# Softmax cross-entropy gradient on one core: rows dealt to partitions 64 at a time instead of 2 at a time

## The chip, the cores and the metric

The kernel runs on one core of one Trainium2 chip. The metric is the device time of one execution in microseconds. Three runs of the kernel before took 1279.22, 1292.99 and 1301.48 us; the median is 1292.99 us.

## The reference

The logits are 8 x 1024 rows of 8192 numbers in fp32 (32 KB a row, 268.4 MB in all), and there is one label for each row. The result is the softmax of each row with 1 taken off at the label's column:

```python
def reference(logits, labels):
    logits_max = np.max(logits, axis=-1, keepdims=True)
    exp_logits = np.exp(logits - logits_max)
    softmax = exp_logits / np.sum(exp_logits, axis=-1, keepdims=True)
    one_hot = np.zeros_like(logits)
    one_hot[batch_idx, seq_idx, labels] = 1.0
    return (softmax - one_hot).astype(np.float32)
```

Every logit is read once and every result written once: 268.4 MB each way.

## The kernel before

**Tiling.** The 8192 rows are cut into 32 blocks (B) of 256 rows. A block holds two rows (G = 2) for each of 128 partitions (P), 64 KB in each partition and 8 MB in all. The tile X has three buffers for blocks (SLOTS), so that one block can be loaded, one worked on and one stored. A column of 128 rows, one in each partition, is called t; there are T = 64 of them, and t = 2b + j is row j of the pair in block b. Which rows of memory a partition gets is said in one place, the views x_b and o_b, in which p is the partition, b the block and j the row of the pair:

```python
x_b = x_nv.rearrange("(b p j) v -> b p j v", p=P, j=G)
o_b = o_nv.rearrange("(b p j) v -> b p j v", p=P, j=G)
```

Here b is the slowest index: a block is 256 consecutive rows, and partition p holds rows 256b + 2p and the one after it, 64 KB that lie together in memory.

**Pieces.** Three strings give, for every block, how it is loaded (LOADS), stored (STORES) and in which order its work is issued (ORDER). A block marked "w" is moved in one transfer of 128 x 64 KB; "r" in two, one for each j, of 128 x 32 KB; "s", for the loads of the first three blocks, in four, which take every second partition of one j. 24 blocks are loaded and 23 stored as "w"; the others are at the two ends.

**Queues.** All loads are issued by SP, but for half of the "s" pieces, which ACT issues at the start. All stores are issued by ACT. The function load waits until the stores from the same buffer, three blocks earlier, have landed; store waits for the last DVE operation of its rows. SP issues only loads, so a load that waits holds up only later loads.

**Work on one t.** row_max takes the negated maximum on DVE. exponentials makes exp(x - max) in place on ACT, with the sum beside it. mark writes a one-hot row of bytes into PSUM (the tile hot) with two ACT operations from the label's column: away is the distance of each group of four columns from the label's group (word), and hot gets the unit of the right byte at distance 0. finish takes the reciprocal of the sum on DVE, and one DVE operation multiplies the row by it and subtracts the bytes. The order is written out by hand in the last loop. All instructions go through the helper run, so the profile gives nearly all of them as line 76 (L76).

**Labels.** Before the first block, ACT's queue loads the labels into 32 partitions, 256 of them each (lab_raw, labels are 64-bit numbers). DVE casts them to fp32 (lab_f), TensorE transposes them twice against an identity matrix that POOL made with a memset and an affine_select, into PSUM (lab_ps, a corner of hot), and DVE casts them back into lab, 128 partitions x 64. From there small DVE operations make word, unit and minus, a column of numbers for each t. POOL's iota makes the column counter count16.

Of the kernel before, what the change touches and what calls it, by code (L numbers as in the profile page):

```python
# [7 lines left out]
P = 128  # L8
G = 2
# [8 lines left out]
def kernel(  # L18
# [6 lines left out]
    nc = tc.nc  # L25
    fp32 = mybir.dt.float32
    i32 = mybir.dt.int32
# [4 lines left out]
    Alu = mybir.AluOpType  # L32

    x_nv = logits.flatten_outer_dims()
    o_nv = out.flatten_outer_dims()
    N, V = x_nv.shape
    T = N // P
    B = T // G
    W = V // 4
    lab_bp = labels.rearrange("a b -> (a b)").rearrange("(b q) -> b q", q=G * P)  # L40
    x_b = x_nv.rearrange("(b p j) v -> b p j v", p=P, j=G)
    o_b = o_nv.rearrange("(b p j) v -> b p j v", p=P, j=G)

    const = ctx.enter_context(tc.tile_pool(name="const", bufs=1))
    psum = ctx.enter_context(tc.tile_pool(name="psum", bufs=1, space=bass.MemoryType.PSUM))

    X = const.tile([P, SLOTS, G, V], fp32)
    lab_raw = const.tile([B, G * P], labels.dtype)
    lab_f = const.tile([B, G, P], fp32)
    ident = const.tile([B, B], fp32)  # L50
    lab = const.tile([P, G, B], i32)
    part = const.tile([P, G, B], i32)
    word = const.tile([P, G, B], fp32)
# [5 lines left out]
    m, s, r = (const.tile([P, T], fp32, name=n) for n in ("m", "s", "r"))  # L59

    hot = psum.tile([P, G, W], i32)
    lab_ps = hot[:, 0, :].bitcast(fp32)[:, :T].rearrange("p (j b) -> p j b", j=G)

    with tc.tile_critical():  # L64
        sem = tc.alloc_semaphore
        got = [[sem(f"got{i}{q}") for q in range(4)] for i in range(SLOTS)]
        put = [[sem(f"put{i}{q}") for q in range(4)] for i in range(SLOTS)]
        lab_got, dve, act, pe, pool = (sem(n) for n in ("lab_got", "dve", "act", "pe", "pool"))
        count = {}

        def run(engine, waits, counter, method, **operands):

            waits = list(dict.fromkeys(waits))
            for w in waits[:-1]:
                engine.wait_ge(*w)  # L75
            instruction = getattr(engine, method)(**operands)  # L76
            for w in waits[-1:]:
                instruction._wait_ge(*w)
            step = 16 if method == "dma_start" else 1
            instruction.then_inc(counter, step)  # L80
            count[counter.name] = count.get(counter.name, 0) + step
            return counter, count[counter.name]
# [20 lines left out]
        def load(b):  # L103
            loaded[b] = []
            before = stored.get(b - SLOTS, [])
            for q, piece in enumerate(PIECES[LOADS[b]]):
                ps, js = piece
                free = [w for other, w in before if meets(piece, other)]
                queue = nc.scalar if LOADS[b] == "s" and ps == halves[1] else nc.sync
                w = run(  # L110
                    queue, free, got[b % SLOTS][q], "dma_start",
                    out=X[ps, b % SLOTS, js, :], in_=x_b[b, ps, js, :],
                )
                loaded[b].append((piece, w))
# [57 lines left out]
                )  # L172
            finished[t] = freed[t] = last

        w_raw = run(nc.scalar, [], lab_got, "dma_start", out=lab_raw[:], in_=lab_bp)
        for b in range(SLOTS):
            load(b)
        w = run(nc.gpsimd, [], pool, "memset", ap=ident[:], constant=0.0)
        w_ident = run(
            nc.gpsimd, [w], pool, "affine_select",  # L180
            out=ident[:], in_=ident[:], compare_op=Alu.not_equal, fill=1.0,
            base=0, pattern=[[-1, B]], channel_multiplier=1,
        )
        w_made = run(
            nc.gpsimd, [], pool, "iota", out=count16[:], pattern=[[1, W]], base=0, channel_multiplier=0
        )
        step = mybir.dt.size(labels.dtype) // 4
        lab32 = lab_raw[:].bitcast(i32).rearrange("b (p j s) -> b j p s", j=G, s=step)
        w_lab = run(nc.vector, [w_raw], dve, "tensor_copy", out=lab_f[:], in_=lab32[:, :, :, 0])
        for j in range(G):  # L190
            w = run(
                nc.tensor, [w_ident, w_lab], pe, "transpose",
                out=lab_ps[:, j, :], in_=lab_f[:, j, :], identity=ident[:],
            )
        w = run(nc.vector, [w], dve, "tensor_copy", out=lab[:], in_=lab_ps)
        w = run(
            nc.vector, [w], dve, "tensor_scalar",
            out=part[:], in0=lab[:], scalar1=2, scalar2=None, op0=Alu.arith_shift_right,
# [3 lines left out]
            out=word[:], in0=part[:], scalar1=-1.0, scalar2=None, op0=Alu.mult,  # L202
        )
        w = run(
            nc.vector, [w_word], dve, "tensor_scalar",
            out=lab[:], in0=lab[:], scalar1=3, scalar2=None, op0=Alu.bitwise_and,
        )
        w = run(
            nc.vector, [w], dve, "tensor_copy", out=minus[:], in_=lab[:]
        )  # L210
        powers = [256.0**k for k in range(4)]
        w = run(
            nc.vector, [w], dve, "tensor_scalar",
            out=unit[:], in0=minus[:], scalar1=0.0, scalar2=powers[0], op0=Alu.is_equal, op1=Alu.mult,
        )
        for k in (1, 2, 3):
            w = run(
                nc.vector, [w], dve, "tensor_scalar",
                out=part[:].bitcast(fp32), in0=minus[:], scalar1=float(k),
                scalar2=powers[k], op0=Alu.is_equal, op1=Alu.mult,  # L220
            )
            w = run(
                nc.vector, [w], dve, "tensor_tensor",
                out=unit[:], in0=unit[:], in1=part[:].bitcast(fp32), op=Alu.add,
            )
        made_dve = run(
            nc.vector, [w], dve, "tensor_scalar",
            out=minus[:], in0=unit[:], scalar1=-1.0, scalar2=None, op0=Alu.mult,
# [77 lines left out]
```

## Time and profile before

| what | value |
|---|---|
| median of three runs | 1292.99 us |
| the profiled execution, its time | 1284.52 us |
| its span, first to last instruction | 1282.7 us |
| DVE busy | 1120.0 us (87%) |
| ACT busy | 722.8 us (56%) |
| packets of the two DMA queues | 98.8% of 16 engines' span |
| moved | 536.98 MB, 419 GB/s over the span |

The profile is of one execution, whose time is 1.8 us longer than its span. Its queue q1 is that of SP, q10 that of ACT. A packet is one run of memory that one of the 16 DMA engines moves: 64 KB for a "w" piece, 32 KB for the others. The DMA share is the time in which packets were under way, as a mean over the 16 engines.

### The profile page before, as it was taken

The numbers are of one execution on the slowest core, as the hardware profiler recorded it, in microseconds if no ns is written. First come the engines' busy times: TensorE is split into PE (matmuls) and PEld (weight loads), VectorE is DVE, ScalarE is ACT, GpSimd is POOL, SyncE is SP. The second block draws the span as 40 slices with busy tenths as digits, with TensorE's granted clock in tenths as the row PEclk, the third lists the DMA queues.
The fourth block names the chain that finished last, engine by engine and source line by source line (L and its number), as shares of the span: only waits on it lengthen the run. The fifth ranks groups of instructions, "written<-read, shape, count | busy, mean of one in ns | idle before, by whom it ended". The sixth has DMA issues, their size and how long they took to land.

```text
span 1282.7 us, 759 instructions
## 1 busy us (share of the span) xinstructions
PE 0.4 (0%) x2; PEld 0.3 (0%) x2; DVE 1120.0 (87%) x207; ACT 722.8 (56%) x257; POOL 2.3 (0%) x7
## 2 busy tenths in 40 slices
PE   0000000000000000000000000000000000000000
PEld 0000000000000000000000000000000000000000
DVE  5999998797979899887997798896799859999995
ACT  2857666456545566544755456563655436656662
POOL 0000000000000000000000000000000000000000
DMA  9999999999989999999999999999999999999999
GB/s 394 425 433 450 425 426 452 425 396 419 454 358 388 441 425 427 425 425 425 425 417 423 380 382 439 442 378 394 425 413 386 443 423 427 410 436 430 436 428 391
DMA packets 11813, 536.98 MB, mean 419 GB/s; under 512 B 1408, under 2 KB 1408, under 8 KB 1440
## 3 DMA queue, kind: packets, MB, share of 16 engines
q10 hardware_dynamic: 6432, 281.09, 51.3%
q1 hardware_dynamic: 5376, 255.86, 47.5%
q14 instruction: 5, 0.04, 0.0%
HBM read 268.50 MB, written 268.44 MB: 419 GB/s over the span
## 4 chain that ended last, share of the span: by engine, by line
DMA 58%; DVE 33%; issue 6%; ACT 1%; DVEq 0%; ACTq 0%; SPq 0%
DMA X<-in_logits_dram 31%; DMA out_dram<-X 28%; DVE m L76 17%; DVE X L76 16%; ACT X L76 1%; DVEq L64 0%; DVE r L76 0%; ACT hot L76 0%; ACT away L76 0%; ACTq L76 0%; DVEq L75 0%; ACTq L301 0%; SPq L64 0%
## 5 line engine op out<-in xcount | busy, mean ns | idle before, releaser
L76 DVE TENSOR_REDUCE m<-X 128x1 f32<-128x8192 f32 x64 | 553.6, 8680 | 142.0 <-DMA X<-in_logits_dram 142.0
L76 ACT ACTIVATE X<-X,m 128x8192 f32<-128x8192 f32 x64 | 455.8, 7121 | 337.5 <-DVE m L76 337.5
L76 DVE SCALAR_TENSOR_TENSOR X<-X,r,hot 128x8192 f32<-128x8192 f32 (+1 forms) x65 | 560.0, 8616 | 3.8 <-ACT hot L76 1.6
L76 ACT ACTIVATE away<-count,word 128x2048 bf16<-128x2048 int16 x64 | 128.1, 2001 | 191.1 <-DVE X L76 149.9
L76 ACT ACTIVATE hot<-away,unit,minus 128x2048 int32<-128x2048 bf16 x64 | 131.9, 2062 | 2.1
L76 ACT ACTIVATION_READ_ACCUMULATOR X<-X,m 128x1 f32 x64 | 11.9, 186 | 0.0
L76 DVE RECIPROCAL r<-s 128x1 f32<-128x1 f32 x64 | 9.9, 154 | 0.0
L76 ACT ACT_TABLE_LOAD x1 | 1.3, 1283 | 5.3 <-issue 5.3
L76 DVE CAST lab_f<-lab_raw 32x256 f32<-32x256 int32 x1 | 0.5, 474 | 2.8 <-DMA lab_raw<-in_labels_dram 2.8
L76 POOL IOTA count<- 128x2048 int16 x1 | 1.8, 1823 | 0.0
L76 DVE TENSOR_TENSOR unit<-unit,part 128x64 f32<-128x64 f32 x3 | 0.7, 224 | 0.1
L76 DVE TENSOR_SCALAR part<-minus 128x64 f32<-128x64 f32 x3 | 0.6, 195 | 0.1
L76 DVE CAST lab<-hot 128x64 int32<-128x64 f32 x1 | 0.2, 225 | 0.5 <-PE hot L76 0.5
L76 PE MATMUL hot<-ident,lab_f 32*128 32x32 f32 x2 | 0.4, 301 | 3.3 <-DVE lab_f L76 3.3
L76 PEld LDWEIGHTS hot<-ident,lab_f 32*128 32x128 f32 x2 | 0.3, 195 | 3.3 <-DVE lab_f L76 3.3
L76 DVE TENSOR_SCALAR part<-lab 128x64 int32<-128x64 int32 x1 | 0.2, 196 | 0.0
L76 DVE TENSOR_SCALAR unit<-minus 128x64 f32<-128x64 f32 x1 | 0.2, 196 | 0.0
L76 DVE TENSOR_SCALAR lab<-lab 128x64 int32<-128x64 int32 x1 | 0.2, 195 | 0.0
L76 DVE TENSOR_SCALAR minus<-unit 128x64 f32<-128x64 f32 x1 | 0.2, 195 | 0.0
L76 DVE TENSOR_SCALAR word<-part 128x64 f32<-128x64 int32 x1 | 0.2, 195 | 0.0
L76 DVE CAST minus<-lab 128x64 f32<-128x64 int32 x1 | 0.2, 194 | 0.0
L76 POOL TENSOR_SCALAR_AFFINE_SELECT ident<-ident 32x32 f32<-32x32 f32 x1 | 0.2, 202 | 0.1
(5 smaller groups left out, 0.5 us busy)
## 6 DMA issues: line engine op xcount, KB each, us to landing
out_dram<-X ACTq DMA_DIRECT2D x18, 4096.0 KB, 30.0
X<-in_logits_dram SPq DMA_DIRECT2D x10, 4096.0 KB, 26.8
X<-in_logits_dram SPq DMA_DIRECT2D x6, 2048.0 KB, 32.8
X<-in_logits_dram ACTq DMA_DIRECT2D x6, 2048.0 KB, 37.3
X<-in_logits_dram SPq DMA_DIRECT2D x24, 42.0
out_dram<-X ACTq DMA_DIRECT2D x23, 42.5
lab_raw<-in_labels_dram ACTq DMA_DIRECT2D x1, 64.0 KB, 1.9
```

Source lines behind the costliest of these rows:

```text
L76: instruction = getattr(engine, method)(**operands)
```

## The change

In the views x_b and o_b the partition becomes the slowest index. Partition p now owns rows 64p to 64p + 63; block b takes rows 64p + 2b and the one after it. A "w" piece still moves 64 KB runs, one in each partition, into the same place of X; in memory the runs of neighbouring partitions lie 64 rows apart instead of 2. As each partition's 64 labels are now consecutive, the labels are loaded straight into 128 partitions, and the cast to fp32, the identity matrix, the transposes and the cast out of PSUM go. One DVE cast, which reads the lower half of each 64-bit label in the order of j and b, makes lab. Everything behind it is the same.

```diff
-    lab_bp = labels.rearrange("a b -> (a b)").rearrange("(b q) -> b q", q=G * P)
-    x_b = x_nv.rearrange("(b p j) v -> b p j v", p=P, j=G)
-    o_b = o_nv.rearrange("(b p j) v -> b p j v", p=P, j=G)
+    lab_pt = labels.rearrange("a b -> (a b)").rearrange("(p t) -> p t", p=P)
+    x_b = x_nv.rearrange("(p b j) v -> b p j v", p=P, j=G)
+    o_b = o_nv.rearrange("(p b j) v -> b p j v", p=P, j=G)
...
-    lab_raw = const.tile([B, G * P], labels.dtype)
-    lab_f = const.tile([B, G, P], fp32)
-    ident = const.tile([B, B], fp32)
+    lab_raw = const.tile([P, T], labels.dtype)
...
-    lab_ps = hot[:, 0, :].bitcast(fp32)[:, :T].rearrange("p (j b) -> p j b", j=G)
...
-        w_raw = run(nc.scalar, [], lab_got, "dma_start", out=lab_raw[:], in_=lab_bp)
+        w_raw = run(nc.scalar, [], lab_got, "dma_start", out=lab_raw[:], in_=lab_pt)
...
-        w = run(nc.gpsimd, [], pool, "memset", ap=ident[:], constant=0.0)
-        w_ident = run(
-            nc.gpsimd, [w], pool, "affine_select",
-            out=ident[:], in_=ident[:], compare_op=Alu.not_equal, fill=1.0,
-            base=0, pattern=[[-1, B]], channel_multiplier=1,
-        )
...
-        lab32 = lab_raw[:].bitcast(i32).rearrange("b (p j s) -> b j p s", j=G, s=step)
-        w_lab = run(nc.vector, [w_raw], dve, "tensor_copy", out=lab_f[:], in_=lab32[:, :, :, 0])
-        for j in range(G):
-            w = run(
-                nc.tensor, [w_ident, w_lab], pe, "transpose",
-                out=lab_ps[:, j, :], in_=lab_f[:, j, :], identity=ident[:],
-            )
-        w = run(nc.vector, [w], dve, "tensor_copy", out=lab[:], in_=lab_ps)
+        lab32 = lab_raw[:].bitcast(i32).rearrange("p (b j s) -> p j b s", j=G, s=step)
+        w = run(nc.vector, [w_raw], dve, "tensor_copy", out=lab[:], in_=lab32[:, :, :, 0])
```

More of the change, by code (lines that the diff above doesn't have):

```diff
@@ L67 @@
         put = [[sem(f"put{i}{q}") for q in range(4)] for i in range(SLOTS)]
-        lab_got, dve, act, pe, pool = (sem(n) for n in ("lab_got", "dve", "act", "pe", "pool"))
+        lab_got, dve, act, pool = (sem(n) for n in ("lab_got", "dve", "act", "pool"))
         count = {}
```

## The prediction

> **What bounds the kernel now.** I read first which engine is full over the whole span: the page's busy line, the rows in 40 slices, and its table of queues.
>
> ```profile
> span 1282.7 us, 759 instructions
> PE 0.4 (0%) x2; PEld 0.3 (0%) x2; DVE 1120.0 (87%) x207; ACT 722.8 (56%) x257; POOL 2.3 (0%) x7
> ...
> DMA  9999999999989999999999999999999999999999
> GB/s 394 425 433 450 425 426 452 425 396 419 454 358 388 441 425 427 425 425 425 425 417 423 380 382 439 442 378 394 425 413 386 443 423 427 410 436 430 436 428 391
> ...
> q10 hardware_dynamic: 6432, 281.09, 51.3%
> q1 hardware_dynamic: 5376, 255.86, 47.5%
> ```
>
> The two queues' packets fill 51.3 + 47.5 = 98.8% of the 16 DMA engines' span; DVE has 13% to spare. So time is bytes through DMA engines. Per engine, q1 (SP: the loads but six) takes 0.475 x 1282.7 = 609 us for 255.86/16 = 15.99 MB, 26.2 GB/s; q10 (ACT: the stores, six loads, the labels) 658 us for 17.57 MB, 26.7 GB/s.
>
> Next, whether this holds in every stage (busy time by window; DMA share and GB/s come last):
>
> ```profile
> 232.00:1008.00 776.00, 0.00 (x0) 0.00 (x0) 663.42 (x114) 432.61 (x154) 0.00 (x0) 1.00 0.98 414
> 1066.00:1260.00 194.00, 0.00 (x0) 0.00 (x0) 191.21 (x34) 124.05 (x44) 0.00 (x0) 1.00 1.00 429
> ```
>
> In the "w" blocks DVE works 663 of 776 us while DMA is at 0.98; in the last "r" blocks DMA (1.00) and DVE (191 of 194 us) are both full. Slower packets would lengthen either stage; faster ones could help only the first. The chain of waits says the same of the "w" blocks: DVE works 35 us on a block, and then a store and the load waiting for its buffer (840 to 930 us) end the chain.
>
> ```profile
> 831.24 8.76 DVE X L76
> 840.00 0.02 issue
> 840.02 47.98 DMA out_dram<-X
> 888.00 0.02 issue
> 888.02 42.01 DMA X<-in_logits_dram
> 930.03 0.02 issue
> 930.05 16.00 DVE m L76 x2
> ```
>
> Last, the packets themselves. The trace's records hold 6016 of 64 KB and 4352 of 32 KB (64 KB for "w" pieces, 32 KB for "r" and "s"). The median 64 KB packet takes 2.42 us, load or store, which is 27.1 GB/s on one engine and 434 on 16. Of the 64 KB loads the slowest twentieth takes 3.20 us or more, of the stores 2.75; the longest packet took 4.86. All excess over the medians is 27.5 us per engine. The DMA rows of the first 16 us, in slices of 0.4 us, show the engines start and end their packets together:
>
> ```profile
> DMA  0000199410990990990990990990990990990590
> ```
>
> **The change, part by part.**
>
> *Labels.* Gone are DVE's cast of 32x256, two transposes on PE and the cast out of PSUM, and POOL's memset and affine_select; one DVE cast of 128x64 takes their place. In the timeline:
>
> ```profile
> 2.80 0.47 DVE L76 CAST lab_f<-lab_raw 32x256 f32<-32x256 int32 x1 [2.80 <-DMA lab_raw<-in_labels_dram]
> ...
> 3.79 0.23 DVE L76 CAST lab<-hot 128x64 int32<-128x64 f32 x1 [0.51 <-PE hot L76]
> ...
> 6.65 0.20 DVE L76 TENSOR_SCALAR minus<-unit 128x64 f32<-128x64 f32 x1
> 15.91 8.69 DVE L76 TENSOR_REDUCE m<-X 128x1 f32<-128x8192 f32 x1 [9.07 <-DMA X<-in_logits_dram]
> ```
>
> The cast (0.47), the wait for PE (0.51) and the second cast (0.23) make 1.2 us, the new cast about 0.23: the chain of labels ends 1.0 us sooner, at 5.9. DVE then waits 9.07 us for the first load, so this is worth nothing. The label transfer is the same 64 KB in 128 packets of 512 B instead of 32 of 2 KB; a 2 KB packet takes 0.08 to 0.19 us, so 8 instead of 2 per engine costs at most 6 x 0.19 = 1.1 us and likely half of it, and a later landing has the same 9 us of cover. Only what delays the first logits packets behind it on ACT's queue reaches the path: 0 to 1.1 us, taken as 0. Without the cover all of it would still be under 2 us. SP issues its 40 loads in the same order, ACT its DMAs and activations too; no wait is added, none taken away, POOL's iota is issued two operations sooner with mark(0) 30 us away.
>
> *Addresses.* A row is 8192 x 4 = 32 KB. Before, partition p of block b starts at row 256b + 2p: neighbours 64 KB apart, the block one stretch of 8 MB. After, it starts at row 64p + 2b: neighbours 64 x 32 KB = 2 MB apart, on loads and on stores. Runs, packet sizes, bytes and counts are the same (24 loads and 23 stores of 128 x 64 KB; the rest 32 KB). The "s" pieces, every second partition, go from 128 KB to 4 MB. So the whole effect is what a packet takes when 16 engines, in step, touch addresses some MB apart instead of some hundred KB.
>
> No row shows a 2 MB step, so it is bounded from both sides. *Nothing:* the nearest row by kind is the first three blocks, 32 KB packets at a 128 KB step: median 1.21 us, as those at 64 KB. A doubled step costs nothing there, but this is a sixteenth of the step in question. *A gain:* at most the 27.5 us of stretched packets. *A loss:* the row for a packet that is held up is the slowest twentieth of the 64 KB loads, 3.20 - 2.42 = 0.78 us over; for a 32 KB packet half, 0.39. Loads: 3072/16 = 192 per engine x 0.78 = 150 us, and 2048/16 = 128 x 0.39 = 50 us: 200 us. Stores: 184 x 0.78 = 144, and 144 x 0.39 = 56: 200 us again. Both: 400 us.
>
> I take the loads alone, 200 us: of the 27.5 us of excess 18.8 is SP's, the loads', so where packets are held up now it is mostly loads, and a run of 64 KB is long enough for engines held up at its start to draw apart before its end. With no spare room on the DMA engines all of it adds to the span. The sum: 1284.5 (the profiled execution: span 1282.7 and 1.8 around it; 8.5 under the median of 1292.99) + 0 for the labels + 200 = **1484 us**.
>
> The Trainium skill, "DMA: Bandwidth & Descriptors", section "Latency and other measured facts", speaks against the change: copies of 128 partitions x 16 KiB between HBM tensors ran at 207 GB/s in each direction with rows 512 KiB apart, at 164 with 2 MiB, at 103 with 4 MiB, and at 214 when padded off the power of two; it infers that streams in step fall on the same HBM channels, and calls that unverified. By it, as an estimate, 268.4 MB each way at 164 GB/s would be 1637 us. This trace's 209 GB/s each way at a 64 KB step agrees with the page's full rate; its runs are four times as long as the page's, and nothing here shows whether this loosens the collision.
>
> **The rivals.**
>
> *B, loads and stores are both held up:* 1284.5 + 400 = 1684 us. For it: both directions get the same step, and in step they alternate in the same rounds, so a late load holds the store behind it. Against: stores are stretched less now (8.8 of 27.5 us). The skill's figure lies between this case and mine.
>
> *C, the step does not matter:* 1284.5 + 0 to 1, say 1285 us. For it: most packets take exactly 2.42 us at 64 KB and the same per byte at a 128 KB step, as if the engine and not the memory set the pace, which leaves an unknown reserve in the memory. Against: engines in step are what a bad step needs, and they are.
>
> *D, faster:* today all 16 engines load from one stretch of 8 MB and store to one; if crowding there stretches packets, partitions that each keep to a region of 2 MB of their own end it. All 27.5 us gone gives 1257 us. It decides if no stretched rounds are left. Against: the stretched rounds stand where one queue has run dry and starts again (near 363 and 402 us), as waits on buffers would make them, and these are unchanged; and the median packet cannot shrink if the engine sets it.
>
> **How the numbers follow.** Forecast A (1484, own range 1310 to 1545, the upper end adding the stores at their own slowest twentieth, 184 x 0.33 = 61 us) 0.44; B 0.22; C 0.24; D 0.10. A step that matters to some degree is what two thirds of the chance stand on; how much is the least known term. About 2% (1267 to 1319) is what a measurement of this kernel can tell from no change; the runs shown spread from 1279 to 1301. Slower: A and B, 0.66; within 2%: C, 0.24; faster: D, 0.10. The range goes from 1267, which leaves out D, to B's 1684, beyond which I leave about 0.08.
>
> **What would show it.** Right: DMA's row still all 9s but GB/s near 360 through the middle; q1's mean 64 KB packet above 3 us, q10's nearly as now; DVE still 1120 us busy, its wait for loads up from 142 us to over 300; the first DVE maximum later than 15.9 us. Wrong: GB/s at 414 to 425 and packets at 2.42 us (C); both queues' packets at 3.2 us (B); a slice row with no dip under 420 (D). The label step is wrong if the last small DVE operation comes after the first load lands.

## The result: 15% slower, and the profile after

The changed kernel's median is 1493.58 us (1466.64 to 1526.58), that of the kernel before 1289.18 us in the runs beside it. The ratio is 1.149, with a 95% interval of 1.124 to 1.174. The profiled execution took 1466.64 us. Here and below medians are over all executions of a kernel, while ratios and their intervals use only those within 1.5% of its fastest in the same group.

The lines of the page that answer to those shown of before (busy time of the engines; DMA share and GB/s in 40 slices; the two queues with packets, MB and share of 16 engines):

```profile
span 1464.9 us, 747 instructions
...
DVE 1119.6 (76%) x206; ACT 722.7 (49%) x257; POOL 2.0 (0%) x5
...
DMA  8999999998999999989999999999899999999997
GB/s 325 405 364 406 415 417 356 358 397 340 369 290 374 365 388 367 387 272 381 387 399 281 347 390 379 337 354 383 336 317 367 385 376 366 345 397 407 398 413 322
...
q1 hardware_dynamic: 5376, 255.86, 49.1%
q10 hardware_dynamic: 6528, 281.09, 48.4%
```

DVE and ACT do the work of before to within 0.4 us. The DMA engines are nearly as full as before (97.5% of the span instead of 98.8%) and move 367 GB/s instead of 419. q1, with the same 5376 packets and bytes, holds an engine for 0.491 x 1464.9 = 719 us instead of 609; q10 for 709 instead of 658. Idle engine time went from 1.2% of the span (15 us) to 2.5% (37 us). Packet time and idle time make up the span, so these three split its growth of 1464.9 - 1282.7 = 182 us: 110 + 51 = 161 us are longer packets, 21 are idle engines.

The same reading by window, and the wait that grew (before, then after):

```profile
230.00:1200.00 970.00, 715.08 (x123) 469.15 (x166) 0.00 (x0) 1.00 0.97 359
1200.00:1400.00 200.00, 176.69 (x31) 111.35 (x40) 0.00 (x0) 1.00 1.00 380
```

```profile
DVE m L76 <- DMA X<-in_logits_dram: 142.0, 25, 13.8
```

```profile
DVE m L73 <- DMA X<-in_logits_dram: 320.0, 25, 30.0
```

The "w" blocks run at 359 GB/s (before: 414) with DVE busy 74% of the time, the last "r" blocks at 380 (before: 429). DVE's wait for loads rose from 142 to 320 us. By the packet records a 64 KB load of SP takes 2.99 us on average (before 2.51), a 64 KB store 2.67 (2.46), a 32 KB load of SP 1.40 (1.22) and a 32 KB packet of ACT's queue 1.29 (1.22). The median store is still at 2.42 us, the median load at 2.85: most loads are stretched, and only a minority of the stores.

The start of the timeline:

```profile
5.73 0.20 DVE L73 TENSOR_SCALAR minus<-unit 128x64 f32<-128x64 f32 x1
...
21.95 8.69 DVE L73 TENSOR_REDUCE m<-X 128x1 f32<-128x8192 f32 x1 [16.02 <-DMA X<-in_logits_dram]
```

The label chain ends at 5.9 us, 0.9 us sooner, and then DVE waits 16.02 us instead of 9.07 for the first logits.

### The profile page after: what moved, and what is told of

It is laid out like the page before. It is cut to its first block, busy times and chain, and to the rows that moved or that the text cites. A ratio compares the mean times of both kernels' runs of the same rounds, so it can differ in the third digit from the quotient of the medians.

```text
span 1464.9 us, 747 instructions
## 1 busy us (share of the span) xinstructions
DVE 1119.6 (76%) x206; ACT 722.7 (49%) x257; POOL 2.0 (0%) x5
## 3 DMA queue, kind: packets, MB, share of 16 engines
q1 hardware_dynamic: 5376, 255.86, 49.1%
## 4 chain that ended last, share of the span: by engine, by line
DMA 36%; another core or an unknown queue 31%; DVE 25%; issue 5%; ACT 1%; DVEq 0%; SPq 0%; ACTq 0%
DMA X<-in_logits_dram 19%; DMA out_dram<-X 17%; DVE X L73 13%; DVE m L73 12%; ACT X L73 1%; DVEq L61 0%; DVE r L73 0%; SPq L73 0%; ACT hot L73 0%; ACT away L73 0%; ACTq L73 0%; DVEq L72 0%; ACTq L286 0%; SPq L61 0%
```

## The experiments

The kernels of one group ran on the same chip beside runs of the kernel before; its median there is given with each group.

### Which part of the change it is (before: 1294.93 us)

**The addresses alone**, in the kernel before:

```diff
-    x_b = x_nv.rearrange("(b p j) v -> b p j v", p=P, j=G)
-    o_b = o_nv.rearrange("(b p j) v -> b p j v", p=P, j=G)
+    x_b = x_nv.rearrange("(p b j) v -> b p j v", p=P, j=G)
+    o_b = o_nv.rearrange("(p b j) v -> b p j v", p=P, j=G)
```

> The kernel before with the changed views of logits and result alone; the labels go the old way (cast, two transposes, cast), so the 1 falls on other rows of the result than in the reference. Theory one, that the 2 MB step between partitions is the whole effect: 1465 to 1525 us, as the changed kernel, SP's 64 KB packets at a mean near 2.99 us. Rival, that the label path (small label packets, a shorter chain) has a part in it: some tens of us less than the changed kernel, or near 1290 if it is the label path alone.

Measured: 1561.84 us, median of four (1520.15 to 1580.25), 267 us over before. The two lines bring the whole loss, and more of it than was expected: only the fastest execution lies in the range of 1465 to 1525, and SP's 64 KB packets took 3.09 us on average. Whether the label path wins something back could not be told across two occasions, so both were run again side by side (below).

**One direction at a time**, in the changed kernel. For the loads alone:

```diff
-    o_b = o_nv.rearrange("(p b j) v -> b p j v", p=P, j=G)
+    o_b = o_nv.rearrange("(b p j) v -> b p j v", p=P, j=G)
```

> The changed kernel with the result stored at the old addresses (64 KB step), so that rows come out in another order; the loads keep the 2 MB step. Theory one in the form of the prediction, that the loads are what is held up: most of the loss stays, 1285 + 130 to 180 = 1415 to 1465 us, SP's packets stretched and ACT's 64 KB packets at 2.42 to 2.50 us. Rival, that loads and stores on the same step collide with each other: under a third of the loss stays, below 1350 us.

Measured: 1380.55 us, median of four (1345.90 to 1392.39), 86 us over before. That is between the two theories; the fastest execution, the only one that a ratio would use, is in the range of the rival.

For the stores alone, the same with x_b:

> The changed kernel with the logits loaded at the old addresses (64 KB step), so that the result's rows hold other rows' values; the stores keep the 2 MB step. If loads are what is held up: at most a quarter of the loss, 1285 to 1335 us, SP's 64 KB packets at a mean of 2.5 to 2.6 us. If the stores' step slows both directions: 1400 us or more, with SP's packets stretched although their own addresses are the old ones.

Measured: 1386.64 us, 92 us over before; ratio 1.091 (1.071 to 1.111). That too is between the two ranges. But SP's 64 KB packets took 2.71 us on average, above the 2.5 to 2.6 of the first theory, and the loss is 92 us where that theory allowed a quarter of it. So the prediction's view that the step holds up loads and leaves stores free is refuted.

The two directions together cost more than their sum. On this chip the medians are 86 us over before for the loads' step, 92 for the stores' step and 267 for both (the addresses alone). By the executions that ratios use it is about 70, 115 and 245, with only one execution that counts for the loads' step and one for both, so the sizes are rough. Some 60 to 90 us, then, appear only when loads and stores have the step at the same time, as the rival of a collision between them has it. As the whole cause that rival is refuted, because each direction also costs something by itself.

The queues of the stores-only change show where the stores' step is paid:

```profile
span 1383.1 us, 747 instructions
...
q10 hardware_dynamic: 6528, 281.09, 51.0%
q1 hardware_dynamic: 5376, 255.86, 47.4%
```

q1's packets take 0.474 x 1383.1 = 656 us an engine, 46 more than before, though the loads' addresses are the old ones; q10's take 705, 47 more. The mean 64 KB load is 2.71 us, the mean store 2.64. About half of what the stores' step adds in packet time shows on the loads that are under way beside them. So a queue whose packets became longer need not be the one whose addresses changed.

**62 rows a partition instead of 64**, with the last 256 rows as one block in the old way:

```diff
-    x_b = x_nv.rearrange("(p b j) v -> b p j v", p=P, j=G)
+    C = 31
+    M = P * C * G
+    x_b = x_nv[:M].rearrange("(p b j) v -> b p j v", p=P, j=G)
+    x_last = x_nv[M:].rearrange("(b p j) v -> b p j v", p=P, j=G)
```

(o_b and the labels likewise; the labels come in two transfers.)

> Each partition owns 62 rows instead of 64 (a step of 1984 KB); the last 256 rows are a block in the old way, and the labels come in two transfers. Theory one, with the power of two as its cause: runs, counts and distance stay, the lower address bits differ between the engines, so the loss is gone: 1275 to 1310 us. Rival, that a step of about 2 MB costs whatever its bits (partitions far apart): 1450 to 1530 us, as the changed kernel.

Measured: 1291.78 us (1286.09 to 1295.74), inside the 1269 to 1302 of before; ratio 1.015 (1.006 to 1.024).

```profile
span 1293.6 us, 748 instructions
...
q10 hardware_dynamic: 6672, 281.09, 50.9%
q1 hardware_dynamic: 5376, 255.86, 47.6%
```

q1 at 616 and q10 at 658 us an engine are nearly back at the values of before (609, 658). Partitions are about as far apart as in the changed kernel (3% less), the runs and packets of logits and result are the same, and the loss is down to 1.5%. So it is not a distance of about 2 MB that costs, but a distance of exactly 2 MB. Of the steps that are no power of two this is the only one that was run.

### The labels, and how the loss grows with the step (before: 1297.76 us)

**The changed kernel and the addresses alone, side by side.**

> The changed kernel once more, on the same chip as the next three. It came out at 1494 us, and its addresses with the old label path at 1562, on another occasion. If the label path is worth nothing, the two agree within 2% here; if the new label path wins back part of the loss, this one is 40 us or more faster.

> The changed addresses with the old label path, the 1 on other rows; beside the changed kernel on one chip. Labels worth nothing: within 2% of it. Labels worth something: 40 us or more slower.

Measured: 1544.69 us (ratio 1.196, 1.183 to 1.209) and 1544.85 us, medians of four each (1531.94 to 1554.05 and 1524.26 to 1570.60). The label path is worth nothing that can be seen in this scatter. The changed kernel's loss itself is 15% on one occasion and 20% on another.

**Smaller powers of two.** With C pairs of rows a partition, in groups of 128 x 2C rows (C is 32 in the changed kernel, 1 before):

```diff
-    x_b = x_nv.rearrange("(p b j) v -> b p j v", p=P, j=G)
+    x_b = x_nv.rearrange("(a p c j) v -> a c p j v", p=P, c=C, j=G)
...
-                    out=X[ps, b % SLOTS, js, :], in_=x_b[b, ps, js, :],
+                    out=X[ps, b % SLOTS, js, :], in_=x_b[b // C, b % C, ps, js, :],
```

> The same work with 16 consecutive rows a partition, four groups of 2048 rows (a step of 512 KB between partitions); labels come straight, in the same way. If the loss grows with the size of the power of two, and most of it comes above 512 KB, as the Trainium skill's DMA page has it for copies (207 GB/s against 164): 1285 to 1340 us. If any large power of two costs the same: 1450 to 1530 us.

> 32 consecutive rows a partition, two groups of 4096 rows (a step of 1 MB). Growing loss: between the steps of 512 KB and 2 MB, 1330 to 1430 us. Same cost for any large power of two: 1450 to 1530 us.

| step between partitions | median us | ratio to before |
|---|---|---|
| 512 KB (C = 8) | 1324.71 | 1.015 (0.998 to 1.033) |
| 1 MB (C = 16) | 1459.17 | 1.128 (1.116 to 1.140) |
| 2 MB (C = 32) | 1544.69 | 1.196 (1.183 to 1.209) |

At 512 KB no loss is shown: the interval includes 1. At 1 MB most of the loss is there, 29 us above the range that a growing loss was given and inside that of the other theory; but that theory is refuted at 512 KB. So the loss sets in between 512 KB and 1 MB, more abruptly than was expected. The Trainium skill, "DMA: Bandwidth & Descriptors", "Latency and other measured facts", has the same order for copies between HBM tensors (207 GB/s a direction at 512 KiB, 164 at 2 MiB). Its figure for 2 MiB, 1637 us as an estimate for this kernel, is beyond what was measured on any occasion (medians of 1494 to 1562).

### One direction by itself, and the length of the runs (before: 1294.42 us)

**Loads only, stores only, at 2 MB.** The loop over blocks is replaced; all pieces are "w":

```diff
+        for b in range(B):
+            row_max(b * G)
+            row_max(b * G + 1)
+            if b + SLOTS < B:
+                stored[b] = [((every, rows), maxed[b * G + 1])]
+                load(b + SLOTS)
```

```diff
+        for b in range(B):
+            t = b * G + 1
+            finished[t] = loaded[b % SLOTS][0][1]
+            if b >= SLOTS:
+                finished[t] = stored[b - SLOTS][0][1]
+            store(t)
```

> The 2 MB step, loads only: all 32 blocks are loaded as 128 x 64 KB runs and DVE takes the two maxima of each (17.4 us a block); no exponentials, no marks, no finish, and only the last block is stored, so the rest of the result stays empty. At 2.42 us a packet the loads take 32 x 8 x 2.42 = 619 us, about 660 us with the first landing and the last store. If the streams of one direction get into each other's way by themselves: packets at a mean of 2.8 us or more, 740 us or more. If it takes loads beside stores: packets at 2.42 to 2.5, 640 to 680 us.

> The 2 MB step, stores only: the first three blocks are loaded and each buffer is then stored 10 or 11 times, as 128 x 64 KB runs, to the 32 blocks of the result, three transfers queued at a time; nothing is computed. At 2.42 us a packet 619 us, about 660 us with the first loads. If one direction is enough: 740 us or more. If it takes loads beside stores: 640 to 680 us.

Measured: 680.98 and 758.57 us. The totals hide the course; GB/s in 40 slices, first of the loads, then of the stores:

```profile
GB/s 312 382 409 401 413 428 432 432 436 428 432 432 428 432 432 432 432 432 436 429 428 432 432 432 432 432 444 432 436 432 432 436 432 432 432 436 432 50 247 247
```

```profile
GB/s 305 329 326 385 326 416 309 371 340 333 378 343 378 364 368 388 385 392 388 402 402 392 406 423 406 427 413 420 434 413 434 440 434 409 437 440 437 406 437 305
```

By their totals the loads meet the second expectation but for 1 us (their packets took 2.46 us on average) and the stores the first. Within the runs both expectations hold in turn. The loads' 64 KB packets that end in the first 40 us take 2.81 us on average, and from 100 us on they run at 2.42 to 2.43. The stores run still holds the three loads up to 121 us. With the loads gone its packets take 2.95 us between 120 and 160 us, 2.84 between 200 and 300, 2.55 between 400 and 500, and 2.44 from 600 on. So one direction is enough to stretch packets, and at the same addresses the stretching fades: for loads in about 100 us, for stores in about 500.

How the 16 engines stand to each other changes meanwhile. As a measure, take in each stretch of two mean packet times the longest pause in which no engine starts a packet. For the loads the median of this pause falls from 1.09 us in the first 40 us to 0.58 between 100 and 200; for the stores from 1.65 us between 125 and 200 to 0.50 between 300 and 400. So the starts spread out while the packets get shorter. But spread-out starts do not by themselves make packets short: between 300 and 600 us the pause is 1.26 us in the kernel before, where most packets take 2.42 us, and 0.65 us in the changed kernel, where most loads take longer. There the stretching does not fade in 970 us of "w" blocks. Whether the other direction keeps it up, or SP's waiting for stores before it can load (1335 us in all in the changed kernel), is not shown.

**Shorter runs.** Both kernels with all pieces as 32 KB runs, but for the first three blocks' loads:

```diff
-LOADS = "sssrrwwwwwwwwwwwwwwwwwwwwwwwwrrr"
-STORES = "rrwwwwwwwwwwwwwwwwwwwwwwwrrrrrrr"
+LOADS = "sssrrrrrrrrrrrrrrrrrrrrrrrrrrrrr"
+STORES = "rrrrrrrrrrrrrrrrrrrrrrrrrrrrrrrr"
```

> The changed kernel with every piece moved in two transfers of 128 x 32 KB (the first three blocks' loads as they were), ORDER as before: the same step of 2 MB, runs half as long. If a long run lets engines draw apart before its end, as the prediction argued, the loss grows: 1600 us or more. If the length of a run does not matter: within 3% of the changed kernel, 1500 to 1590 us, set against the next kernel's change.

> The same pieces of 32 KB runs in the kernel before (64 KB step), to see what the pieces themselves cost: all theories say within 2% of before, 1275 to 1320 us.

Measured: the changed kernel so cut takes 1320.89 us, ratio to before 1.022 (1.016 to 1.028); the kernel before so cut 1248.70 us, ratio 0.966 (0.959 to 0.973). Both lie below every range that was expected. The middle of the two, by window and by queue, first with the 2 MB step, then with 64 KB:

```profile
232.00:1008.00 776.00, 668.48 (x117) 431.48 (x156) 0.00 (x0) 1.00 1.00 415
```

```profile
q10 hardware_dynamic: 9840, 281.09, 50.1%
q1 hardware_dynamic: 8832, 255.86, 49.2%
```

```profile
232.00:1008.00 776.00, 0.00 (x0) 0.00 (x0) 703.11 (x121) 455.85 (x162) 0.00 (x0) 1.00 1.00 433
```

```profile
q10 hardware_dynamic: 9744, 281.09, 52.3%
q1 hardware_dynamic: 8832, 255.86, 47.6%
```

At 2 MB the middle runs at 415 GB/s with shorter pieces, against 359 with long ones; the step still costs 1320.89 - 1248.70 = 72 us. Of the 70 us between the two spans 54 are on SP's queue, where a 32 KB load takes 1.33 us on average instead of 1.22, 8 on ACT's, and 8 are idle engines. At 64 KB the middle goes from 414 to 433 GB/s, the rate of back-to-back packets: hardly any packet is stretched (2 us of excess over the median an engine, instead of 27.5 in the kernel before). A "w" piece cut in two changes two things, the run and the moment at which half a block is stored or its buffer released. These two runs do not separate them. The second kernel beats both kernels of this study and computes the whole result.

## Why the prediction was right

**What bounds the kernel: right.** The DMA engines are full before and nearly full after, DVE and ACT work as long as before, and longer packets lengthened the span by all they grew: 161 of its 182 us. The other 21 us are idle engines, which the sum had at nothing.

**Labels at nothing: right**, in the chain (0.9 us sooner; 1.0 was worked out) and in the whole (1544.69 against 1544.85 us). The first maximum comes 6 us later, and that is the loads' step: it starts at 21.95 us in the changed kernel, at 22.12 with the old label path (the addresses alone), and at 16.25 with the new label path and the loads at the old addresses (the stores-only change).

**The size of the step: right in the sum, wrong in its parts, and the sum by luck.** 1484 was predicted and 1494 measured, but 1545 on another occasion, and 1562 for the addresses alone on a third. The sum put 200 us on the loads and none on the stores. In the profile after, 110 us are on SP's queue, 51 on ACT's and 21 idle. The failed step is "I take the loads alone": the old excess lay on the loads, and that was read as whose addresses matter. The runs with one direction changed show 70 to 86 us for the loads' step, 92 to 115 for the stores' step, and 60 to 90 more when both have it. What made the total fit is that 0.78 us for every load was too much (2.99 - 2.51 = 0.48 us was measured), which about made up for the stores at nothing.

**"A run of 64 KB is long enough for engines held up at its start to draw apart": not borne out.** With runs of half the length most of the loss went away instead of growing. (The pieces were also stored and released earlier, so the run's length is not shown to be the reason.) Where the engines' starts were seen to spread out, in a stream of one direction, it took 100 us and more and not one run. And "in step" describes the kernel before better than the middle of the changed kernel, by the pauses given above.

**Rival B** had the stores in it, rightly, and its argument that a late load holds up the store behind it fits the part that only both directions show. But at the full 0.78 us it is 190 us too long beside 1494, 140 beside 1545 and 122 beside 1562. **Rival C** is refuted at 2 MB; a step of 512 KB still shows no loss, so its argument from 64 and 128 KB was sound as far as it went. **Rival D** is refuted by the packets, which became longer. That the stretched rounds can be taken out of the kernel was right, by other means: with 32 KB pieces it took 1249 us, near the 1257 that D had.

**The signs.** The middle at 359 GB/s (near 360 was said), DVE's wait at 320 us (over 300), the first maximum at 21.95 us (after 15.9), the mean load at 2.99 us (just under the 3 given). Wrong: stores "nearly as now"; they rose from 2.46 to 2.67. And the DMA row is no longer all 9s, as more of the engines' time is idle.

## What to carry to other kernels

When a layout gives partitions rows that lie a large power of two apart, change the step by a little before anything else: 62 rows instead of 64 took the loss from 15 to 20% down to 1.5% here, at the same run length. Where a layout costs DMA time, change one direction at a time: the queue with long packets need not be the one with the bad addresses, and what the two directions cost need not add up. And longer transfers are not better by themselves: here a 32 KB packet takes 1.21 us and a 64 KB packet 2.42, the same per byte, and pieces of half the size won 3.4% in the kernel before, by the shorter run or by the earlier release of half a block.

## What was not expected of the hardware

- Stretched packets at a 2 MB step fade in a stream of one direction: loads alone come to 2.42 us a packet in some 100 us, stores alone fall from 2.95 us to 2.44 in some 500 us. With loads and stores in turn the middle stays at 359 GB/s, and at 331 on the second occasion.
- The steps of the two directions do not add up: 86 and 92 us one at a time, 267 together on the same chip (medians).
- A 2 MB step on the stores lengthens loads at untouched addresses: 656 us an engine for SP's queue instead of 609.
- The scatter goes with the addresses and pieces: with 32 KB pieces and a 64 KB step four runs lay within 0.2 us of each other (1248.55 to 1248.74), while the kernel before ranged over 22 us on the same chip, and the changed kernel from 1467 to 1554 over two occasions.
- Still open: what in the address makes packets long at 1 MB and 2 MB and not at 512 KB or 1984 KB, why the changed kernel's loss is 15% on one occasion and 20% on another, and whether the shorter run or the earlier release of half a block is what helps in the last two runs.
